# A replicated bias strip written to DRAM in sixteen pieces between the weight chunks, from a work buffer

## The chip, the core and the metric

The kernel runs on one core of a Trainium2 chip. The metric is the device time of one execution in microseconds (us). The kernel before takes 1424.04 us, the median of 3 runs (1423.84 to 1424.34).

## What is computed

The reference is a decoder trunk of two layers on 256 tokens of width 1024, all in float32. A layer has a SwiGLU feed forward, a token mixer and a second feed forward, each followed by a layer norm. The mixer runs sliding-window attention beside a gated delta rule. The change touches one input of the attention: a bias by the distance between query and key, looked up from a table of 32 buckets by 16 heads.

```python
pos_bias = jnp.transpose(rel_bias[t5_bucket(band_rel())], (2, 0, 1)).astype(jnp.float32)
for i in range(DEPTH):
    x = layernorm(DN_ALPHA * x + 0.5 * swiglu(x, ffn_w13[i, 0], ffn_w2[i, 0]), ln_g[i, 0], ln_b[i, 0])
    y = hybrid_mixer(x, w_in[i], ..., pos_bias)
    x = layernorm(DN_ALPHA * x + y, ln_g[i, 1], ln_b[i, 1])
    x = layernorm(DN_ALPHA * x + 0.5 * swiglu(x, ffn_w13[i, 1], ffn_w2[i, 1]), ln_g[i, 2], ln_b[i, 2])
# in the mixer's attention, for a block of 128 queries and 256 keys:
s = jnp.einsum('bqkgd,bskd->bkgqs', qi, ki) + bias
```

## The kernel before

**The weights.** All weights pass through the core once, in 219 chunks of 1 MB (128 partitions by 2048 floats), c0, c1, c2 and so on. c0 to c21 are the first product of layer 0's first feed forward, c22 to c32 its second product, and from c33 on the mixer's. A chunk is loaded by one DMA (L277, in `load_next`; c0 by four), all issued by SP. ACT then rounds it into a high part (CAST, in quarters of 512 columns) and DVE makes the low part, the rest (TENSOR_TENSOR); PE makes each product from three single-pass matmuls of these parts. In the first product a chunk takes 48 matmuls of 256 columns; when they are through, ACT evacuates the bank (ACTIVATE, silu).

**The order of the work.** A Python scheduler writes the instructions of each engine in a fixed order while it keeps its own estimate of each engine's time. Small chains of instructions (generators) are let in between groups of large products. Every engine works through its own list in order, and the waits between engines are semaphores. All DMAs stand in the one list of SP, and so in one hardware queue. `load_next` runs up to three chunks ahead of the conversion and takes its buffer from a pool of 20 slots; another pool, `a`, has 6 work buffers of 1024 columns, which only the mixer uses.

**The strip.** `setup_bias` is such a chain, spawned right after the input has been transposed. It loads the bias table and a one-hot matrix into a buffer `s`, lets PE multiply them, and lets DVE copy the result to a row `r` of 384 columns on 16 partitions, one for each head. Then one DMA (L624) writes `r` 128 times for each head into a DRAM tile `rdram`, at a pitch of 385: 2048 rows of 1536 bytes, 3 MB. Read back at a pitch of 384, each query's row has moved by one. The readers are `att_pair` in the mixer (L1272), two DMAs for each pair of heads, in both layers. In the kernel before `s` is a slot, and the strip is one DMA.

Of the kernel before, what the change touches and what calls it, by code (L numbers as in the profile page):

```python
# [15 lines left out]
P = 128  # L16
# [20 lines left out]
PARTS = 4    # a weight chunk is split in so many steps  # L37
# [4 lines left out]
# column offsets of w_in  # L42
# [3 lines left out]
# head order of the query tiles: a tile holds one head of each partition half  # L46
# [3 lines left out]
def mixer_plan():  # L50
    """Order of the weight chunks of the mixer: (kind, index)."""
    plan = [("z", 0), ("z", 1), ("va", 0)] + [("qa", c) for c in range(5)]
    plan += [(w[:-1], int(w[-1])) for w in ORDER.split()]
    plan += [("wo", c) for c in range(4)]
    return plan
# [18 lines left out]
class Engine:  # L74
    """Issues instructions on one engine and keeps an estimate of when it is through with them.

    Every method takes, first, the estimated time at which its operands are there, and returns the
    estimated time at which its result is. The estimates only settle the order of issue.
    """
# [4 lines left out]
    def __getattr__(self, name):  # L84
        fn, cost = getattr(self.eng, name), self.cost

        def issue(t, *args, **kw):
            fn(*args, **kw)  # L88
            out = kw.get("out", args[0] if args else None)
            self.t = max(self.t, t) + cost(name, out, args, kw)  # L90
            # another function means another table, but for the plain ones
            if name == "activation" and args[2] not in (AF.Copy, AF.Square, self.table):
                self.table = args[2]
                self.t += 1.3
            return self.t + 0.15

        return issue
# [30 lines left out]
class Co:  # L128
    """A chain of small instructions, issued piecemeal between the large products."""
# [5 lines left out]
class Kern:  # L135
    NA = 3      # chunks done one token tile at a time where a phase begins
    LAG = 4     # chunks by which token tile 1 is behind at the end of the second product

    def __init__(self, ctx, tc, a, out):
# [39 lines left out]
        self.lows = deque()  # L179

# [21 lines left out]
    def acq(self, *kinds, dt=F32):  # L202
        """For chains: all of these buffers at once, as soon as they are free."""
        need = {k: kinds.count(k) for k in kinds}
        while any(len(self.pools[k]) < n for k, n in need.items()):
            yield None
        got = [self.new(k, dt) for k in kinds]
        return got[0] if len(got) == 1 else got

    def take(self, kind):  # L210
        """For the main line."""
        self.until(lambda: self.pools[kind])
        return self.new(kind)
# [10 lines left out]
    def tick(self):  # L224
        """Between two groups of large products: whatever small work is ready by now, in turn."""
        ready = [co for co in self.cos if co.wake <= self.T.t]
        n = 0
        while ready:
            again = []
            for co in ready:  # L230
                try:
                    w = next(co.gen)
                except StopIteration as e:
                    co.live, co.end = False, e.value or 0.0
                    self.cos.remove(co)
                    continue
                if w is not None:
                    co.wake = w
                    if w <= self.T.t:
                        again.append(co)  # L240
            ready = again
            n += 1
            assert n < 1000
        self.pump()
# [15 lines left out]
    def after(self, *cos):  # L260
        """For chains: until these others are through."""
        while any(co.live for co in cos):
            yield None
        return max(co.end for co in cos)
# [6 lines left out]
    def load_next(self):  # L271
# [3 lines left out]
        for j in range(n):  # L275
            f = slice(j * SLOT // n, (j + 1) * SLOT // n)
            self.nc.sync.dma_start(out=s[:, f], in_=self.a["wstream"][i, :, f])  # L277
        if self.plan[i][0] == "va":
            self.nc.sync.dma_start(out=self.xps[0], in_=self.a["va7"][self.plan[i][1]])
# [8 lines left out]
    def conv_hi(self):  # L288
        """First operand of the next part of the next chunk."""
# [25 lines left out]
    def pump(self, force=False):  # L315
        i, q = self.ci, self.cp
        n = len(self.plan)
        # two free slots are kept for the split of the next chunk
# [10 lines left out]
    def chunk(self, key):  # L329
        """The two operands of a weight chunk, which is now in use."""  # L330
# [5 lines left out]
    def need(self, key, at):  # L336
        """The chunk is there up to and with this column."""
# [21 lines left out]
    def full_B(self, key, xh, xl):  # L359
        """ps[col, tok] for two column tiles: weights stationary."""  # L360
# [12 lines left out]
    def full_A(self, key, t, n=256):  # L373
        """ps[tok, 0:n]: activations of token tile t stationary, weights moving."""
# [17 lines left out]
    def split(self, t, hi, lo, src):  # L392
        """hi + lo = src, both as single pass operands."""
# [16 lines left out]
    def xT_half(self, tok, q, t):  # L410
        """Transpose and split four column tiles of x."""
# [16 lines left out]
    def ln(self, tok, acc, c, half, last=False):  # L428
        """x[tok] = layernorm(alpha * x[tok] + alpha * c * acc), then its transpose."""
# [48 lines left out]
    def up_A(self, ps, hh, hl):  # L478
        """Evacuates a chunk done for one token tile: silu, gate, transpose."""
# [26 lines left out]
    def ffn(self, l, f, ln_i, first, last):  # L506
# [6 lines left out]
        # the middle group is the short one: it is through before the last chunks of the second product  # L513
# [46 lines left out]
        # token tile 1 is behind in the last chunks, so that the norm of tile 0 is hidden  # L560
# [47 lines left out]
    def setup_bias(self):  # L608
        """Relative bias as a Toeplitz strip in DRAM: R[h, n] = bias at rel = 255 - n."""
        nc = self.nc  # L610
        s = self.alloc()
# [10 lines left out]
        # row q of a head starts 385 * q in: read back at a pitch of 384, it has moved right by q  # L622
        self.rd = self.p_dram.tile([NH_A, P, 385], F32, name="rdram")
        nc.sync.dma_start(out=self.rd[:, :, 0:384], in_=r.unsqueeze(1).broadcast_to([NH_A, P, 384]))  # L624
        self.release(s)


class Mixer:
# [11 lines left out]
    def run(self):  # L640
# [23 lines left out]
        # gates of the norm, and values with the inputs of the decay, one token tile at a time  # L664
# [25 lines left out]
        # the scaled queries take the place of the keys and values of the attention  # L690
# [3 lines left out]
        # sliding window attention  # L694
# [10 lines left out]
        def go(name, *deps):  # L705
            """Spawns a chain as soon as everything that it needs has been issued."""
# [88 lines left out]
    def branch_b(self, c, banks):  # L795
        """Adds the part of four heads to [column, token] of four column tiles.

        Two column tiles share a bank, as one group of accumulation: its start clears the bank, whose
        other columns, marked as not yet written, are overwritten by their first product.
        """  # L800
# [78 lines left out]
    def decay(self):  # L879
# [21 lines left out]
        # log(1 + e) = 2 atanh(y), y = e / (2 + e) <= 1/3  # L901
# [3 lines left out]
        n = 8  # L905
# [11 lines left out]
        # running sums inside each token tile, and the last one of the first  # L917
# [60 lines left out]
    def tok4(self, t, u, tr):  # L978
        """[tok, (t, h), channel] of two heads."""
# [90 lines left out]
    def inverse(self, deps):  # L1070
# [5 lines left out]
        # a partition holds one block: [column half v, row], of the even or the odd columns  # L1076
# [37 lines left out]
        # merge pairs of 32, then the two of 64; U = T^T  # L1114
# [108 lines left out]
    def solved(self, *cos):  # L1223
        """The space of the delta rule goes to the weights."""
# [38 lines left out]
    def att_pair(self, m, *deps):  # L1263
        """Heads 2m and 2m + 1."""
# [4 lines left out]
        # bias: [r, head, own | previous | own]  # L1269
# [24 lines left out]
        # nm = -max(scores, sink), for the two query tiles  # L1294
# [41 lines left out]

def _t5_onehot():
    """[bucket, n]: bucket of the relative distance 127 - n."""
# [11 lines left out]
def _stack_k(w, cols):  # L1350
    """[1024, n] -> [128, 8 * n] with the contraction index on partitions."""
    w = w[:, cols]
    return w.reshape(KD, P, -1).transpose(1, 0, 2).reshape(P, -1)


def _rows(w, c):
    """Two row tiles of a [k, 1024] matrix -> [128, 2048]."""
# [65 lines left out]
```

## Time and profile before

| what | value |
|---|---|
| median of 3 runs | 1424.04 us |
| the profiled execution's span | 1421.5 us |
| PE (matmuls) | 1388.3 us, 98% of the span |
| DVE | 953.7 us, 67% |
| ACT | 754.5 us, 53% |
| DMA queue of the kernel | 245.55 MB, 50.1% of 16 engines |
| the strip, one DMA | 3072.0 KB, 32.8 us from issue to landing |
| granted TensorE clock, mean of the span | 0.99 |

The span is the time from the first to the last instruction of one profiled execution; 2.5 us of the median lie outside it. In the views, PE is the matmul side of TensorE and PEld its weight loads, SPq is SP's own list, and a releaser behind "<-" is what ended an idle time. Nearly all engine instructions carry line L88, since one helper issues them, so they are told apart by operation and tile: `slot<-in_wstream_dram` is a load of weights, `slot<-slot` on ACT the high part, `slot<-slot,slot` on DVE the low part, `bank<-slot,slot` a product, `w<-bank` the evacuation of a chunk of the first product.

### The profile page before, as it was taken

The numbers are of one execution on the slowest core, as the hardware profiler recorded it, in microseconds if no ns is written. First come the engines' busy times: TensorE is split into PE (matmuls) and PEld (weight loads), VectorE is DVE, ScalarE is ACT, GpSimd is POOL, SyncE is SP. The second block draws the span as 40 slices with busy tenths as digits, with TensorE's granted clock in tenths as the row PEclk, the third lists the DMA queues.
The fourth block names the chain that finished last, engine by engine and source line by source line (L and its number), as shares of the span: only waits on it lengthen the run. The fifth ranks groups of instructions, "written<-read, shape, count | busy, mean of one in ns | idle before, by whom it ended". The sixth has DMA issues, their size and how long they took to land.

```text
span 1421.5 us, 26161 instructions
## 1 busy us (share of the span) xinstructions
PE 1388.3 (98%) x10590; PEld 1316.4 (93%) x10590; DVE 953.7 (67%) x2016; ACT 754.5 (53%) x1740; POOL 38.4 (3%) x36
## 2 busy tenths in 40 slices
PE   8599999999999999999999999999999999999997
PEld 7599989889999989999899998898999999899986
DVE  4355567886997696555575555778779778855554
ACT  4344444677566754444444444457774577444441
POOL 0000000000000100000000000000000010000000
PEclk9799999999999999999999999999999999999999
DMA  7964554245533475545654455534444316554560
GB/s 220 255 214 148 207 212 169 98 155 176 186 120 119 144 252 198 179 151 205 237 201 155 151 205 207 194 113 145 170 169 160 135 60 251 204 197 150 183 231 30
DMA packets 46264, 247.21 MB, mean 174 GB/s; under 512 B 5280, under 2 KB 16064, under 8 KB 17856
## 3 DMA queue, kind: packets, MB, share of 16 engines
q1 hardware_dynamic: 46144, 245.55, 50.1%
q8 instruction: 83, 1.36, 0.4%
q14 instruction: 37, 0.30, 0.1%
HBM read 241.34 MB, written 4.19 MB: 173 GB/s over the span
## 4 chain that ended last, share of the span: by engine, by line
PE 95%; DMA 3%; DVE 1%; ACT 0%; SPq 0%; issue 0%; DVEq 0%; ACTq 0%
PE bank L88 95%; DMA slot<-in_wstream_dram 3%; DVE slot L88 1%; ACT slot L88 0%; SPq L591 0%; ACT w L88 0%; DVE bn_st L88 0%; DVEq L1419 0%; DVE w L88 0%; SPq L588 0%; DVE bn_mv L88 0%; DVE bn_rs L88 0%; DVE bd L88 0%; SPq L624 0%; ACTq L88 0%
## 5 line engine op out<-in xcount | busy, mean ns | idle before, releaser
L88 PE MATMUL bank<-slot,slot 128*128 128x256 f32 (+3 forms) x9268 | 1299.1, 300 | 19.9 <-ACT slot L88 18.2
L88 PEld LDWEIGHTS bank<-slot,slot 128*128 128x128 f32 (+1 forms) x9268 | 1212.4, 192 | 82.4 <-ACT slot L88 19.1
L88 DVE TENSOR_TENSOR slot<-slot,slot 128x512 fp32r<-128x512 f32 (+1 forms) x880 | 564.4, 684 | 121.3 <-ACT slot L88 111.1
L88 ACT CAST slot<-slot 128x512 fp32r<-128x512 f32 x872 | 489.1, 619 | 176.5 <-PE bank L88 103.6
L88 ACT ACTIVATE w<-bank 128x256 f32<-128x256 f32 (+1 forms) x97 | 35.4, 365 | 243.8 <-PE bank L88 243.5
L88 DVE TENSOR_TENSOR w<-w,bank 128x256 f32<-128x256 f32 (+1 forms) x97 | 38.4, 396 | 182.1 <-ACT w L88 181.7
L88 ACT CAST slot<-bank 128x512 fp32r<-128x512 f32 (+2 forms) x58 | 24.4, 429 | 51.4 <-PE bank L88 51.3
L88 PE MATMUL bank<-a,slot 128*128 128x128 f32 (+4 forms) x576 | 49.5, 255 | 0.0
L88 PEld LDWEIGHTS bank<-a,slot 128*128 128x128 f32 (+3 forms) x576 | 41.3, 145 | 4.8 <-issue 0.3
L88 DVE TENSOR_TENSOR slot<-bank,slot 128x128 fp32r<-128x128 f32 (+3 forms) x66 | 33.7, 511 | 16.7 <-ACT slot L88 16.5
L88 DVE SCALAR_TENSOR_TENSOR w<-bank,convw,w 128x255 f32<-128x255 f32 (+2 forms) x96 | 41.0, 473 | 2.7 <-ACT w L88 2.4
L88 ACT COPY slot<-bank 128x512 f32<-128x512 f32 (+1 forms) x30 | 16.7, 558 | 47.4 <-PE bank L88 47.4
L88 DVE TENSOR_TENSOR slot<-w,slot 128x256 fp32r<-128x256 f32 x79 | 33.6, 425 | 10.4 <-ACT slot L88 0.7
L88 DVE TENSOR_TENSOR a<-a,a 128x126 f32<-128x126 f32 (+22 forms) x124 | 35.5, 286 | 2.5
L88 DVE SCALAR_TENSOR_TENSOR slot<-bank,slot 128x512 f32<-128x512 f32 x24 | 16.6, 690 | 29.0 <-PE bank L88 28.8
L88 POOL TENSOR_TENSOR bn_rs<-bn_rs,expo 128x1 f32<-128x1 f32 x12 | 11.2, 937 | 869.8 <-DVE bn_rs L88 869.8
L88 ACT ACTIVATE junk<-bank 128x128 f32<-128x128 f32 x96 | 26.6, 277 | 12.4 <-PE bank L88 9.7
L88 ACT CAST slot<-w 128x256 fp32r<-128x256 f32 x79 | 32.0, 405 | 0.6 <-DVE w L88 0.6
L88 ACT COPY a<-bank 128x384 f32<-128x384 f32 (+3 forms) x40 | 20.0, 504 | 20.6 <-PE bank L88 20.5
L88 ACT ACTIVATE a<-a,a_nm 128x128 f32<-128x128 f32 x64 | 28.3, 448 | 4.2 <-DVE a_nm L88 4.2
L88 DVE SCALAR_TENSOR_TENSOR slot<-bank,convw,slot 128x255 f32<-128x255 f32 (+2 forms) x48 | 20.5, 475 | 11.2 <-ACT slot L88 11.2
L88 ACT ACTIVATE slot<-bank 128x256 f32<-128x256 f32 (+2 forms) x22 | 9.7, 440 | 30.5 <-PE bank L88 30.1
(108 smaller groups left out, 564.5 us busy)
## 6 DMA issues: line engine op xcount, KB each, us to landing
slot<-in_wstream_dram SPq DMA_DIRECT2D x215, 1024.0 KB, 4.9
slot<-in_ln_gb_dram SPq DMA_DIRECT2D x6, 1024.0 KB, 6.8
a<-rdram SPq DMA_DIRECT2D x16, 256.0 KB, 4.6
rdram<-slot SPq DMA_DIRECT2D x1, 3072.0 KB, 32.8
a<-rdram SPq DMA_DIRECT2D x16, 128.0 KB, 4.4
slot<-in_x_dram SPq DMA_DIRECT2D x4, 256.0 KB, 3.8
slot<-in_wstream_dram SPq DMA_DIRECT2D x4, 256.0 KB, 6.3
out_dram<-slot SPq DMA_DIRECT2D x4, 256.0 KB, 2.1
```

The costliest lines, as they stand in the source:

```text
L88: fn(*args, **kw)
```

## The change

`setup_bias` takes `s` from the pool of work buffers instead of the slots. It no longer issues the strip: it puts 16 calls into a list, `spread`. Each writes 8 of the 128 rows of every head, 128 rows of 1536 bytes or 192 KB. `load_next` issues one of these calls behind the load of each odd chunk for as long as there are any. The last one gives `s` back. The kernel's other lines in the diff are comments taken out.

```diff
         self.lows = deque()
+        self.spread = deque()
...
             self.nc.sync.dma_start(out=s[:, f], in_=self.a["wstream"][i, :, f])
+        if self.spread and i % 2:
+            self.spread.popleft()()
         if self.plan[i][0] == "va":
...
     def setup_bias(self):
         nc = self.nc
-        s = self.alloc()
+        s = yield from self.acq("a")
         rb, oh, r = s[0:NUM_BUCKETS, 0:NH_A], s[0:NUM_BUCKETS, 128:256], s[0:NH_A, 512:896]
...
         self.rd = self.p_dram.tile([NH_A, P, 385], F32, name="rdram")
-        nc.sync.dma_start(out=self.rd[:, :, 0:384], in_=r.unsqueeze(1).broadcast_to([NH_A, P, 384]))
-        self.release(s)
+
+        n = P // 16
+
+        def piece(q):
+            nc.sync.dma_start(out=self.rd[:, q:q + n, 0:384], in_=r.unsqueeze(1).broadcast_to([NH_A, n, 384]))
+            if q + n == P:
+                self.release(s)
+
+        self.spread += [lambda q=q: piece(q) for q in range(0, P, n)]
```

The lists of PE, DVE, ACT and POOL hold the same instructions in the same order in both kernels; only buffer numbers, and slot against `a` for the strip's operands, differ. SP's list alone changes. Its place at the strip, in the kernel before (slot_211 is c4, slot_261 is c5, and so on up to c11):

```order
L614 DMA slot_139<-in_onehot_dram 32x128
L277 DMA slot_211<-in_wstream_dram 128x2048
L624 DMA rdram<-slot_139 2048x1x384
L277 DMA slot_261<-in_wstream_dram 128x2048
L277 DMA slot_302<-in_wstream_dram 128x2048
L277 DMA slot_356<-in_wstream_dram 128x2048
L277 DMA slot_407<-in_wstream_dram 128x2048
L277 DMA slot_473<-in_wstream_dram 128x2048
```

The same place now (L278 is the load of a chunk, slot_211 is c4, slot_260 is c5; L631 is a piece):

```order
L617 DMA a_139<-in_onehot_dram 32x128
L278 DMA slot_211<-in_wstream_dram 128x2048
L278 DMA slot_260<-in_wstream_dram 128x2048
L631 DMA rdram<-a_139 16x8x384
L278 DMA slot_302<-in_wstream_dram 128x2048
L278 DMA slot_356<-in_wstream_dram 128x2048
L631 DMA rdram<-a_139 16x8x384
L278 DMA slot_408<-in_wstream_dram 128x2048
L278 DMA slot_474<-in_wstream_dram 128x2048
L631 DMA rdram<-a_139 16x8x384
```

c5 has moved ahead of all writing of the strip, and behind it stands a sixteenth of the strip before c6 and c7, and so on by pairs.

Where the pieces end, at the start of the mixer, SP's list before reads as follows (slot_1929 is c35, the values' chunk, with its last columns in spill_w; `a_2467` is the first read of the strip):

```order
L277 DMA slot_1898<-in_wstream_dram 128x2048
L277 DMA slot_1929<-in_wstream_dram 128x2048
L279 DMA spill_w<-in_va_dram 128x272
L277 DMA slot_1984<-in_wstream_dram 128x2048
L277 DMA slot_2026<-in_wstream_dram 128x2048
L645 DMA convw<-in_conv_w_dram 128x96
L647 DMA vec<-in_vec_dram 128x32
L650 DMA dng<-in_vec_dram 128x1
L277 DMA slot_2082<-in_wstream_dram 128x2048
L277 DMA slot_2227<-in_wstream_dram 128x2048
L277 DMA slot_2258<-in_wstream_dram 128x2048
L1272 DMA a_2467<-rdram 128x2x128
```

And now (slot_1943 is c35):

```order
L278 DMA slot_1912<-in_wstream_dram 128x2048
L278 DMA slot_1943<-in_wstream_dram 128x2048
L631 DMA rdram<-a_139 16x8x384
L282 DMA spill_w<-in_va_dram 128x272
L278 DMA slot_1999<-in_wstream_dram 128x2048
L278 DMA slot_2041<-in_wstream_dram 128x2048
L655 DMA convw<-in_conv_w_dram 128x96
L657 DMA vec<-in_vec_dram 128x32
L660 DMA dng<-in_vec_dram 128x1
L278 DMA slot_2097<-in_wstream_dram 128x2048
L278 DMA slot_2242<-in_wstream_dram 128x2048
L278 DMA slot_2273<-in_wstream_dram 128x2048
```

The sixteenth piece stands behind c35 and ahead of its last columns; the first read of the strip follows nine DMAs later, as the next row.

## Rows read from the trace of the kernel before

**Rows 1.** The page: span, PE, granted clock, chain by engine, two DMA issues

```profile
span 1421.5 us, 26161 instructions
PE 1388.3 (98%) x10590; PEld 1316.4 (93%) x10590; DVE 953.7 (67%) x2016; ACT 754.5 (53%) x1740; POOL 38.4 (3%) x36
...
PE 95%; DMA 3%; DVE 1%; ACT 0%; SPq 0%; issue 0%; DVEq 0%; ACTq 0%
...
slot<-in_wstream_dram SPq DMA_DIRECT2D x215, 1024.0 KB, 4.9
...
rdram<-slot SPq DMA_DIRECT2D x1, 3072.0 KB, 32.8
```

**Rows 2.** Chain that ended last, in order: start us, length us, what

```profile
22.84 0.08 SPq L624
22.93 0.04 issue
22.97 35.35 DMA slot<-in_wstream_dram
...
58.39 0.63 ACT slot L88
...
59.06 170.92 PE bank L88 x1168
```

**Rows 3.** Timeline of PE and ACT, 20 to 92: start, us, instruction, [idle before <-releaser]

```profile
21.84 20.42 PE L88 MATMUL bank<-slot,slot 128*128 128x256 f32 x168
59.06 33.12 PE L88 MATMUL bank<-slot,slot 128*128 128x256 f32 x255 [16.80 <-ACT slot L88]
...
30.78 0.38 ACT L88 ACTIVATE w<-bank 128x256 f32<-128x256 f32 x1 [1.96 <-PE bank L88]
58.39 1.14 ACT L88 CAST slot<-slot 128x512 fp32r<-128x512 f32 x2 [27.23 <-DMA slot<-in_wstream_dram]
...
84.65 0.38 ACT L88 ACTIVATE w<-bank 128x256 f32<-128x256 f32 x1 [2.94 <-PE bank L88]
...
90.41 0.38 ACT L88 ACTIVATE w<-bank 128x256 f32<-128x256 f32 x1 [3.00 <-PE bank L88]
```

**Rows 4.** Stretches: length, busy PE PEld DVE ACT POOL, PEclk, DMA share, GB/s

```profile
9.80:18.70 8.90, 8.90 (x50) 8.68 (x51) 4.68 (x8) 4.77 (x7) 0.00 (x0) 1.00 1.02 424
25.00:42.20 17.20, 17.20 (x144) 17.05 (x143) 5.39 (x10) 4.19 (x9) 0.00 (x0) 1.00 0.90 102
42.30:59.00 16.70, 0.00 (x0) 0.00 (x0) 0.00 (x0) 0.61 (x2) 0.00 (x0) 0.63 0.93 194
59.00:62.00 3.00, 2.94 (x12) 2.72 (x13) 2.83 (x5) 3.00 (x8) 0.00 (x0) 0.50 1.02 431
62.00:65.00 3.00, 3.00 (x20) 3.00 (x19) 3.00 (x7) 2.72 (x7) 0.00 (x0) 0.69 1.00 423
65.00:68.00 3.00, 3.00 (x27) 3.00 (x26) 3.00 (x7) 2.23 (x6) 0.00 (x0) 1.00 1.01 426
...
80.00:160.00 80.00, 80.00 (x666) 79.90 (x665) 46.27 (x83) 37.98 (x84) 0.00 (x0) 1.00 0.52 183
160.00:230.00 70.00, 70.00 (x352) 59.60 (x351) 45.62 (x76) 31.64 (x60) 1.98 (x2) 1.00 0.54 188
```

**Rows 5.** SP's own list, 0 to 23; c4's landing us; SP's longest wait

```profile
10.41 0.35 SPq L277 DMA_DIRECT2D slot<-in_wstream_dram  x1
22.26 0.67 SPq L624 DMA_DIRECT2D rdram<-slot  x1
22.97 8.94 SPq L277 DMA_DIRECT2D slot<-in_wstream_dram  x1
...
DMA to landing us min/median/max: 11.2/11.2/11.2
...
SPq L624 <- DVE slot L88: 11.8, 1, 11.8
```

**Rows 6.** Loads of c29, c30, c33 alone: ns, issued at; landing us; ACT's casts

```profile
L277 SPq DMA_DIRECT2D slot<-in_wstream_dram x1: 327/327/327, 173.7 to 173.7; - x1
...
L277 SPq DMA_DIRECT2D slot<-in_wstream_dram x1: 327/327/327, 179.1 to 179.1; - x1
...
DMA to landing us min/median/max: 4.8/4.8/4.8
...
L277 SPq DMA_DIRECT2D slot<-in_wstream_dram x1: 327/327/327, 192.2 to 192.2; - x1
...
DMA to landing us min/median/max: 5.1/5.1/5.1
...
186.53 2.19 ACT L88 CAST slot<-slot 128x512 fp32r<-128x512 f32 x4 [0.94 <-PE bank L88]
...
197.41 4.27 ACT L88 CAST slot<-slot 128x512 fp32r<-128x512 f32 x8 [3.26 <-PE bank L88]
```

**Rows 7.** SP at c35's last columns; reads of the strip: ns, first and last start

```profile
200.96 0.43 SPq L279 DMA_DIRECT2D spill_w<-in_va_dram  x1
...
L1272 SPq DMA_DIRECT2D a<-rdram x32: 359/462/905, 228.7 to 989.5; - x32
```

**Rows 8.** Loads of the input, four of 256 KB: first and last start, landing us

```profile
L591 SPq DMA_DIRECT2D slot<-in_x_dram x4: 420/432/432, 1.2 to 2.6; - x4
...
DMA to landing us min/median/max: 3.2/3.8/4.4
```

## The prediction, on record before the changed kernel ran

> **What bounds the kernel now.** I read the page first. PE is busy for 98% of the span, and 95% of the chain that ended last is PE [rows 1]. So nothing on DVE, ACT or SP is worth anything by itself; only a stretch in which PE stands still can be taken out, and the 3% of DMA in the chain is the one place where another resource holds the end. The strip is the odd row among the DMA issues: 3072 KB in 32.8 us, where a chunk of weights of 1024 KB lands in 4.9 us [rows 1]. The chain in order of time shows where the two meet: SP issues the strip (L624), issues the load of c5 right behind it at 22.97, and that load takes 35.35 us; ACT casts at 58.39 and PE goes on at 59.06 [rows 2]. All DMAs stand in one queue, so c5 waited behind the strip.
>
> PE's timeline shows what that cost: its matmuls of c1 to c4 run to 42.26 (21.84 + 20.42), and then it is idle for 16.80 us until ACT has a quarter of c5 [rows 3]. ACT itself stood for 27.23 us with a cast of c5 at the head of its list [rows 3]. That PE worked on for so long is owed to c1 to c4, which were in SBUF by then.
>
> The stretches add a second loss. While PE stands, the granted clock falls to a mean of 0.63; in the 3 us after it, it is 0.50, which is the lower of the two levels (1.2 against 2.4 GHz), then 0.69, and from 65 on 1.00 [rows 4]. So c5 and a part of the chunks behind it ran at half the speed. After that PE is busy for all of 80 to 230 at 1.00 [rows 4], and the chain has 170.92 us of PE from 59.06 without a break [rows 2]. Whatever time is taken out ahead of 65 should therefore move the whole rest of the program forward.
>
> **What the stall costs in all.** The evacuations are the best clock: ACT's ACTIVATE of a chunk follows the chunk's last matmul. In the undisturbed part they stand 5.76 us apart (90.41 - 84.65) [rows 3]. The one at 30.78 is c2's and the one at 90.41 is c9's, counted in the timeline. Seven chunks at 5.76 are 40.32 us; they took 59.63. The excess is 19.31 us: 16.80 of gap, and 2.51 of low clock. The second part agrees with the stretches: 3 us at 0.50 and 3 us at 0.69 lose 1.5 + 0.9 = 2.4 us.
>
> **The change part by part.**
>
> *c5 goes ahead.* The strip's DMA waited 11.8 us for DVE's copy of `r`, with c5's load behind it [rows 5]. In the new order c5 stands ahead of the first piece. c4 was issued at 10.41 [rows 5]; c5 follows it, and at the 424 GB/s of that stretch [rows 4] its 1.05 MB take 2.5 us of the queue behind c4, which landed at 21.6 (10.4 + 11.2) [rows 5]. It will be there by some 25, and at a pace of 5.76 its cast is due behind c2's evacuation, at about 31. So the gap goes: -16.80. PE then never stands, the clock has no reason to fall: -2.51.
>
> *What is late next.* c6 and c7 stand behind the first piece, which still waits for DVE until 22.26 [rows 5]. A piece is a sixteenth of the strip: 32.8 / 16 = 2.05 us of the queue. c6 lands by about 22.97 + 2.05 + 4.9 = 30 and is cast at about 31 + 5.76 = 36.8, so 7 us to spare; each chunk behind it gains, as the queue moves two chunks and a piece in 2 x 2.47 + 2.05 = 7.0 us (1.05 MB at 424 GB/s is 2.47) while PE needs 11.52 for the two. Neither ends the gap anew.
>
> *Sixteen pieces beside the weights.* They are 15 issues more in SP's list, at 0.67 us as the strip's took [rows 5]; SP has nothing else to do there. Their 32.8 us of queue time do not go away, they are spread to c35, which was issued just ahead of its last columns at 200.96 [rows 7]. The DMA engines are taken 0.52 and 0.54 of that time by now [rows 4]; 32.8 us in some 160 make it 0.73. A piece costs PE something only where a chunk lands less than 2.05 us before its cast. I took issue, landing and cast for each chunk from c9 on; the two tightest are c30 (179.1 + 4.8 = 183.9, cast at 186.53: 2.6 us) and c33 (192.2 + 5.1 = 197.3, its casts being the second half of the row of eight, at about 199.5: 2.2 us) [rows 6]. c33 has c32 between itself and a piece. c30 stands straight behind one in SP's list, but is issued 5.4 us after c29 (173.7) [rows 6], while c29 needs 2.47 of the queue and the piece 2.05. So neither should see even the 2.05. Cost: 0, with the bound taken below.
>
> *The reads of the strip.* The first one is issued at 228.7 [rows 7], some 28 us after c35. The last piece needs 2 us of queue and its landing, so the wait for it is over in time. Cost 0. The same cover holds if all moves forward by 19 us, as both do.
>
> *The work buffer.* `s` in pool `a` is held to c35; the pool's users are in the mixer, and the lists of PE, DVE, ACT and POOL are the same instruction by instruction. The pool of slots has one more free for a while, which moves only the numbers. Cost 0.
>
> **Small transfers.** The four input loads of 256 KB, issued within 1.4 us, land 3.2 to 4.4 us after their issue [rows 8]: the last one 2.6 us behind the first, so 0.87 us apart, although one by itself takes 3.2. Start and end of neighbours overlap. The Trainium skill, DMA: Bandwidth & Descriptors, section Rules for kernel authors, asks for at least 1 MiB in a DMA and speaks against pieces of 192 KB. If that held here as time in the queue, a piece would hold it for 2.05 us and also for the part of an input load's 3.2 us that is no transfer (3.2 less 0.62 at 424 GB/s, 2.6), 4.65 in all. c30 and c33 would then be late by up to 4.65 - 2.6 = 2.05 and 4.65 - 2.2 = 2.45; other chunks have more room. Sum by that: 4.5 us given back. I take 0, by the input loads' spacing, and keep 4.5 for the range.
>
> **The sum.** The profiled span is 1421.5, the median 1424.04; the 2.5 us outside it are not touched. 1421.5 - 19.3 = 1402.2 of span, and 1424.04 - 19.3 = **1404.7 us**.
>
> **The rivals.**
>
> 1. *The gap goes and the clock doesn't come back*, because PE meets a shorter wait at c5 or c6 that lets it fall all the same. Only 16.8 us are gained at the most: 1407.2. Against it stands the 6 to 7 us in which c5 and c6 are early.
>
> 2. *Pieces hold the queue with their ends*, as worked out above: 1404.7 + 4.5 = 1409.2. Against it: the spacing of the input loads.
>
> 3. *The pieces fill the queue: slower.* The strip was one DMA of 2048 rows, a piece is 16 by 8 rows. If a piece is spread over fewer of the 16 DMA engines than the strip was, it takes longer. Two chunks leave 11.52 - 4.95 = 6.57 us of the queue, so a piece up to 6.57 us is hidden. From there each further us costs 16; at 7.8 us the whole gain is gone. On a quarter of the engines a piece would take 8.2 us, and the loss would be 16 x 1.63 = 26.1: 1430.8. Against it: the strip ran at 102 GB/s with a DMA share of 0.90 [rows 4], so all engines took part although its source has 16 partitions, and a piece still has 16 heads outermost.
>
> 4. *No change*: PE would have starved anyhow, for want of weights rather than for the strip. The weights came at 102 GB/s less the strip, that is hardly at all, from 25 to 42, and at 431 as soon as it was through [rows 4]; PE needs 1.05 MB in 5.76 us, 182 GB/s. I see nothing for it.
>
> **How the numbers follow.** Forecast 1404.7: 0.83. Rival 1: 0.06. Rival 2: 0.06. Rival 3: 0.03. Rival 4: 0.02. The upper end of the range takes in rivals 1 and 2: 1409.2. The lower end: the clock's loss is a single observation, and without a profile it may last twice as long; then the gain is 2.5 more: 1402.2. A measurement of this kernel can tell about 0.2%, 2.8 us, from no change. Faster by more than that: 0.83 + 0.06 + 0.06 = 0.95; the same 0.02; slower 0.03.
>
> **What would show it.** In the profile of the changed kernel, PE's matmuls from 21.84 have no idle of more than a us before the mixer, and PEclk is 1.00 from 10 to 230. The evacuations stand 5.76 apart from 25 on, and c9's comes at about 71.1. c5 lands by about 25. Sixteen rows `rdram<-a` of 192 KB stand among the DMA issues, each landing in 3 to 7 us; the DMA share is about 0.7 from 80 to 180. The first read of the strip is issued at about 209, without a wait. The span is about 1402. I am wrong if PE waits for a chunk behind a piece (c6, c30 or c33 first), if a piece takes over 6 us of the queue, or if PE is slower in the same matmuls.

## The result, and the profile after

The changed kernel takes 1403.21 us (median of 4 runs, 1401.87 to 1406.20) where the kernel before takes 1423.94 in the same runs: a ratio of 0.9862, with an interval of 0.9850 to 0.9874 (the two medians alone give 0.9855). The forecast was 1404.7, a ratio of 0.9864. Repeated on another occasion the ratio was 0.9874 (0.9857 to 0.9890).

The page's lines that answer to [rows 1], and the issues of strip and weights:

```profile
span 1400.7 us, 26179 instructions
PE 1383.9 (99%) x10590; PEld 1312.0 (94%) x10590; DVE 954.9 (68%) x2016; ACT 753.8 (54%) x1740; POOL 39.6 (3%) x36
...
PE 98%; DVE 1%; DMA 0%; ACT 0%; issue 0%; SPq 0%; DVEq 0%
...
slot<-in_wstream_dram SPq DMA_DIRECT2D x215, 1024.0 KB, 5.0
...
rdram<-a SPq DMA_DIRECT2D x16, 192.0 KB, 5.5
```

DMA, 3% of the chain before, is at 0%. The sixteen pieces land 5.5 us after their issue in the median, about as long as a chunk five times their size: each stands right behind one, and from c11 on lands 0.5 to 1.0 us after it. The timeline of PE and ACT for the stretch of [rows 3]:

```profile
21.46 172.78 PE L88 MATMUL bank<-slot,slot 128*128 128x256 f32 x1224
...
30.40 0.38 ACT L88 ACTIVATE w<-bank 128x256 f32<-128x256 f32 x1 [1.96 <-PE bank L88]
30.68 1.13 ACT L88 CAST slot<-slot 128x512 fp32r<-128x512 f32 x2
...
64.96 0.38 ACT L88 ACTIVATE w<-bank 128x256 f32<-128x256 f32 x1 [2.94 <-PE bank L88]
...
70.72 0.38 ACT L88 ACTIVATE w<-bank 128x256 f32<-128x256 f32 x1 [3.00 <-PE bank L88]
```

PE runs for 172.78 us from 21.46 on without a break, and ACT's first cast of c5, which had waited to 58.39, starts at 30.68. The evacuations of c2 and c9 are 40.32 us apart, seven times 5.76 exactly, where before they were 59.63 [rows 3]: the 19.31 us are all gone. The stretches of [rows 4] (length, busy PE PEld DVE ACT POOL, PEclk, DMA share, GB/s):

```profile
25.00:42.20 17.20, 17.20 (x146) 17.20 (x144) 11.66 (x21) 9.17 (x21) 0.00 (x0) 1.00 0.90 331
42.30:59.00 16.70, 16.70 (x142) 16.70 (x140) 10.04 (x18) 8.01 (x18) 0.00 (x0) 1.00 0.60 204
59.00:62.00 3.00, 3.00 (x28) 3.00 (x26) 2.10 (x5) 2.74 (x6) 0.00 (x0) 1.00 0.52 164
...
80.00:160.00 80.00, 80.00 (x589) 76.50 (x588) 44.76 (x79) 36.88 (x78) 0.00 (x0) 1.00 0.57 193
160.00:210.00 50.00, 50.00 (x264) 43.02 (x263) 34.80 (x58) 22.60 (x43) 1.98 (x2) 1.00 0.61 208
```

The granted clock is 1.00 in all five. From 25 to 42 the queue moves 331 GB/s, weights and pieces, where it moved the strip alone at 102 [rows 4]. The profiled spans differ by 20.8 us, 1.5 more than the stall. The chains of the two traces say where that comes from. The mixer of layer 1, in the kernel before and in the changed one (start us, length us):

```profile
923.05 306.06 PE bank L88 x2567
```

```profile
903.33 304.52 PE bank L88 x2567
```

The same 2567 matmuls took 1.54 us longer in the one profiled execution of the kernel before; that belongs to the execution and not to the change (the last section). The execution after also starts 0.4 us earlier, and has 0.5 us more behind the last piece of its chain, which cancel. Over the runs the gain is 1.4% and 1.3%, 18 to 21 us.

### The profile page after: what moved, and what is told of

Its sections match the earlier page's. It is cut to its first block, busy times and chain, and to the rows that moved or that the text cites. A ratio compares the mean times of both kernels' runs of the same rounds, so it can differ in the third digit from the quotient of the medians.

```text
span 1400.7 us, 26179 instructions
## 1 busy us (share of the span) xinstructions
PE 1383.9 (99%) x10590; PEld 1312.0 (94%) x10590; DVE 954.9 (68%) x2016; ACT 753.8 (54%) x1740; POOL 39.6 (3%) x36
## 3 DMA queue, kind: packets, MB, share of 16 engines
q1 hardware_dynamic: 46384, 245.55, 49.8%
## 4 chain that ended last, share of the span: by engine, by line
PE 98%; DVE 1%; DMA 0%; ACT 0%; issue 0%; SPq 0%; DVEq 0%
PE bank L88 98%; DVE slot L88 1%; DMA slot<-in_x_dram 0%; ACT slot L88 0%; SPq L594 0%; ACT w L88 0%; DVE bn_st L88 0%; DVEq L1429 0%; DVE w L88 0%; SPq L591 0%; DVE bn_mv L88 0%; DVE bn_rs L88 0%; DVE bd L88 0%
## 5 line engine op out<-in xcount | busy, mean ns | idle before, releaser
L88 ACT CAST slot<-bank 128x512 fp32r<-128x512 f32 (+2 forms) x58 | 24.3, 428 | 51.8 <-PE bank L88 51.7
L88 DVE SCALAR_TENSOR_TENSOR slot<-bank,slot 128x512 f32<-128x512 f32 x24 | 16.6, 690 | 28.9 <-PE bank L88 28.8
L88 DVE SCALAR_TENSOR_TENSOR slot<-bank,convw,slot 128x255 f32<-128x255 f32 (+2 forms) x48 | 20.5, 475 | 11.1 <-ACT slot L88 11.1
```

## The experiments

**The two ties.** In the kernel before, the strip holds c5 twice. c5's load stands behind it in SP's queue. And c5's high part goes into the very slot from which the strip is read, since that slot was given back when the strip had been issued; ACT's list shows a wait for the strip's DMA ahead of that cast. The change cuts both. Three kernels cut one or both, with the strip in a single DMA in each.

*awhole*: the work buffer alone.

```diff
-        s = self.alloc()
+        s = yield from self.acq("a")
```

> One part alone: the kernel before with the strip's operands in a work buffer instead of a slot; the strip is still one DMA of 3 MB ahead of c5 on SP. In the kernel before, ACT's first cast of c5 waits on c5's landing and also on the strip's, since the high part of c5 goes into the slot that the strip is read from. Theory 1 (the queue decides): c5 still lands at about 58, the gap of 16.8 us stays, 1424 us. Theory 2 (the buffer decides): the cast goes on sooner, 1405 us.

Measured: 1424.39 us, ratio 1.0008 (0.9998 to 1.0017). Theory 1. The queue's tie is enough to keep the whole stall. ACT's longest wait up to 80 (us in total, times, longest):

```profile
ACT slot L88 <- DMA slot<-in_wstream_dram: 30.4, 2, 28.0
```

And PE's timeline:

```profile
60.21 20.04 PE L88 MATMUL bank<-slot,slot 128*128 128x256 f32 x149 [17.56 <-ACT slot L88]
```

*actq_slot*: the queue alone. ACT issues the strip on its own DMA queue, still from the slot.

```diff
-        nc.sync.dma_start(out=self.rd[:, :, 0:384], in_=r.unsqueeze(1).broadcast_to([NH_A, P, 384]))
+        nc.scalar.dma_start(out=self.rd[:, :, 0:384], in_=r.unsqueeze(1).broadcast_to([NH_A, P, 384]))
```

> The kernel before with the strip issued by ACT, on its own DMA queue, still as one DMA and still from a slot. The weights are no longer behind it in the queue. Theory 1 (only the queue mattered): c5 lands by about 30, PE never stands, 1404 us. Theory 2 (the slot mattered too): ACT's cast of c5 still waits until the strip has been read from the slot it writes, at 55 or later, as the weights now share the engines with it; the gap of some 13 to 17 us stays, 1418 to 1424 us.

Measured: 1423.78 us, ratio 1.0003 (0.9993 to 1.0012). Theory 2. Its trace, first c5's load alone (ns, issued at; landing us):

```profile
L277 SPq DMA_DIRECT2D slot<-in_wstream_dram x1: 346/346/346, 11.8 to 11.8; - x1
...
DMA to landing us min/median/max: 12.5/12.5/12.5
```

The strip's issue among the DMA issues, then ACT's longest wait, then PE's timeline:

```profile
rdram<-slot ACTq DMA_DIRECT2D x1, 3072.0 KB, 35.8
```

```profile
ACT slot L88 <- DMA rdram<-slot: 26.9, 1, 26.9
```

```profile
59.23 20.94 PE L88 MATMUL bank<-slot,slot 128*128 128x256 f32 x152 [16.51 <-ACT slot L88]
```

c5 is in SBUF at 24.3 (11.8 + 12.5), 34 us earlier than before, and it is of no use: ACT waits 26.9 us for `rdram<-slot`, and PE stands for 16.51 us as ever. Before, the two waits ended within 4 us of each other (the strip landed at 22.26 + 32.8 = 55.1, c5 at 58.3), and a view that names the last releaser showed the second alone.

*actq_a*: both edits together.

> The kernel before with the strip as one DMA, issued by ACT on its own queue, and its operands in a work buffer: neither queue nor slot ties the weights to it, and nothing is cut into pieces. Theory 1 (the stall is the tie of c5 to the strip, not the strip's size): 1403 to 1406 us, as the changed kernel. Theory 2 (a strip in one go starves the weights on the shared DMA engines whichever queue it is in): a chunk of weights needs 10 us or more while it runs, PE waits again, 1412 to 1424 us.

Measured: 1404.21 us, ratio 0.9872 (0.9857 to 0.9887). Theory 1: the changed kernel's time, with nothing cut into pieces. PE's timeline, and the DMA issues from 20 to 70:

```profile
22.42 57.86 PE L88 MATMUL bank<-slot,slot 128*128 128x256 f32 x480
```

```profile
slot<-in_wstream_dram SPq DMA_DIRECT2D x8, 1024.0 KB, 15.1
...
rdram<-a ACTq DMA_DIRECT2D x1, 3072.0 KB, 38.3
```

On PE's row there is no gap from 22.42 to 80, where the view ends. Between 20 and 70 us a chunk needs 15.1 us to land, since it shares the engines with the strip, but it moves, and PE's lead covers it. The Trainium skill says in DMA: Bandwidth & Descriptors, section Issuing engines are not separate DMA queues, that issuing on several engines saves only the time of issue. These runs differ: *awhole* and *actq_a* differ in the issuing engine alone, and take 1424.39 and 1404.21 us. What ACT's queue took away was the order within one queue; from a slot (*actq_slot*) it saved nothing.

**How fine the pieces must be.** The changed kernel with another count (`n = P // 1`, `// 2` and `// 4` for 16), work buffer and place kept.

> The changed kernel with the strip in one piece instead of sixteen, behind c5, operands in the work buffer. Theory (the queue passes nothing until the strip is through): the strip is issued at about 22 and through at about 55, c6 lands at about 58; PE is through with c5 at 47.7, so it stands for 11 us, and the clock falls again for 2.5: 1403 to 1405 and 13.5 is 1417 to 1418.5 us. Rival (c5 ahead of the strip and the work buffer are all that counts, the cutting nothing): 1403 to 1405 us.

Measured: 1419.6 us, ratio 0.9975 (0.9965 to 0.9986).

> The changed kernel with the strip in two pieces of 16.4 us of the queue, behind c5 and c7. By the queue's own times: the first piece runs from about 22 to 38, c6 lands at 42 and c7 at 44, both before PE is through with c5 at 47.7; the second piece holds the queue to 61, c8 lands at about 63.5, and PE needs it at 47.7 + 2 x 5.76 = 59.2. Theory (a piece costs what it exceeds the lead of the load behind it): a gap of some 4 to 5 us at c8 and 1 to 3 us of catching up, 1409 to 1413 us. Rival (the weights queued behind any long DMA are late by all of it): two gaps, over 1415 us. Rival (two pieces are as good as sixteen): 1402 to 1406 us.

Measured: 1410.4 us, ratio 0.9908 (0.9891 to 0.9925).

> The changed kernel with the strip in four pieces of 8.2 us of the queue, behind c5, c7, c9 and c11. By the same times c6 lands at about 33, c8 at 47 and c10 at 60, where PE needs them at 47.7, 59.2 and 70.7. Theory (the lead of the loads decides): no gap, 1402 to 1406 us, as with sixteen. Rival (pieces must be no longer than the 6.6 us that two chunks leave of the queue): late loads at c8 or c10, 1407 us or more.

Measured: 1403.97 us, ratio 0.9864 (0.9850 to 0.9879). PE's rows behind c5 with one piece, with two, and with four:

```profile
58.63 31.57 PE L88 MATMUL bank<-slot,slot 128*128 128x256 f32 x238 [12.04 <-ACT slot L88]
```

```profile
62.95 0.51 PE L88 MATMUL bank<-slot,slot 128*128 128x256 f32 x2 [3.24 <-ACT slot L88]
63.68 36.58 PE L88 MATMUL bank<-slot,slot 128*128 128x256 f32 x290 [0.22 <-DVE slot L88]
```

```profile
21.12 69.14 PE L88 MATMUL bank<-slot,slot 128*128 128x256 f32 x574
```

The gaps are 12.0, 3.2 and 0. The theory holds for the gaps in all three: PE stands when a piece exceeds the lead of the load behind it, and about as long (some 1 us more than worked out with one piece, 1 us less with two). The whole loss is larger, 15.6 and 6.4 us against four pieces, so 3 to 4 us more are lost with each gap. With two pieces the granted clock fell there, as behind the stall of the kernel before:

```profile
62.00:65.00 3.00, 1.83 (x9) 1.62 (x9) 1.93 (x4) 2.72 (x7) 0.00 (x0) 0.82 1.01 426
65.00:68.00 3.00, 3.00 (x18) 3.00 (x18) 3.00 (x7) 2.72 (x8) 0.00 (x0) 0.62 1.02 426
```

How much of this is the clock was not tried here; *warm* below tries it for the kernel before. One piece still gains 0.25% on the kernel before, which is what c5's place ahead of the strip is worth, with the work buffer. By the runs the cutting is worth 14 to 16 us, and four pieces do what sixteen do.

**What a piece costs.** *x4* writes four times as much behind each odd chunk.

```diff
+            m = 3 * n
+            nc.sync.dma_start(out=more[:, 3 * q:3 * q + m, 0:384], in_=r.unsqueeze(1).broadcast_to([NH_A, m, 384]))
```

> The changed kernel with four times the writing: behind each piece a second DMA of 16 by 24 rows from the same operands into a DRAM tile that nobody reads, so that each odd chunk is followed by 768 KB. Theory of the prediction (two chunks leave 6.57 us of the queue, a piece below that is free, beyond that each us costs one per pair): 8.2 us a pair is 1.6 too much, 26 us over the sixteen pairs, less the lead of 12 to 18 us by which loads land before their casts: 1411 to 1420 us. Rival (the queue has more room than that): 1402 to 1406 us. Rival (each piece in the way costs PE its whole time): 98 us more of the queue, over 1480 us.

Measured: 1404.47 us, ratio 0.9872 (0.9859 to 0.9886): the second theory, more room than I gave it. Two stretches (columns as above), ACT's casts of c28 to c34, and the two kinds of piece among the DMA issues:

```profile
80.00:160.00 80.00, 80.00 (x587) 76.39 (x587) 44.30 (x78) 36.90 (x78) 0.00 (x0) 1.00 0.89 244
150.00:190.00 40.00, 40.00 (x178) 33.14 (x177) 22.84 (x38) 17.38 (x32) 0.00 (x0) 1.00 0.96 273
```

```profile
161.08 4.27 ACT L88 CAST slot<-slot 128x512 fp32r<-128x512 f32 x8 [3.26 <-PE bank L88]
169.19 2.19 ACT L88 CAST slot<-slot 128x512 fp32r<-128x512 f32 x4 [3.85 <-DMA slot<-in_wstream_dram]
171.73 2.19 ACT L88 CAST slot<-slot 128x512 fp32r<-128x512 f32 x4 [0.35 <-PE bank L88]
180.20 4.48 ACT L88 CAST slot<-slot 128x512 fp32r<-128x512 f32 x8 [6.28 <-DMA slot<-in_wstream_dram]
191.30 2.18 ACT L88 CAST slot<-slot 128x512 fp32r<-128x512 f32 x4 [6.62 <-DMA slot<-in_wstream_dram]
```

```profile
more<-a SPq DMA_DIRECT2D x16, 576.0 KB, 11.0
rdram<-a SPq DMA_DIRECT2D x16, 192.0 KB, 9.1
```

The queue is full: 0.89 and 0.96 of the engines' time. From c30 on ACT waits for the weights themselves, 3.9 to 6.6 us at a time, so the lead of the loads is used up. c30's cast comes at 169.19 and came at 166.84 in the changed kernel. Yet PE is busy for all of 150 to 190: the casts are made that much ahead of PE's need. The 1411 to 1420 us of the first theory did not come, and the trace shows that the piece was taken too large. ACT waits for c30, c32 and c34 and casts them as they land, at 169.19, 180.20 and 191.30: a pair takes 11.0 to 11.1 us of the full queue, not 13.15 (4.95 + 8.2). Less the two chunks' 4.95, that is 6.1 us for 768 KB, under the 6.57 that the prediction leaves a piece. So its threshold was not passed here; larger pieces and longer strips were not tried.

**The slot and sixteen pieces.** *slot* is the changed kernel with `s = self.alloc()` again.

> The changed kernel with the strip's operands in a slot again, in sixteen pieces as before. No weight's operand is written into that slot while pieces are read from it, since it is given back behind c35 only; instead the weights have one slot less for 180 us, and some loads and casts move a place in their lists. Theory 1 (the work buffer matters for a strip in one go alone): 1402 to 1406 us. Theory 2 (with pieces, the missing slot makes loads late): 1408 us or more.

Measured: 1405.22 us, ratio 0.9876 (0.9863 to 0.9890). Theory 1. With pieces the slot is given back behind c35 only, no weight is written into it while it is read, and one slot less for the weights costs nothing that these runs can tell.

**The clock's share.** *warm* keeps PE busy in the stall of the kernel before.

```diff
         wh, wl = self.chunk(key)
+        if key == ("w13", 0, 0, 5):
+            b = self.take("co")
+            for i in range(136):
+                self.nc.tensor.matmul(b[:, 0:256], lhsT=xh[:, i % KD, 0:P], rhs=xh[:, i % KD, :], start=True, stop=True)
+            self.release(b)
```

> The kernel before, with 136 matmuls of 128x256 more on PE between c4 and c5, on operands that have long been there and into a bank that nobody reads; 136 at 0.12 us fill 16.3 of the 16.8 us in which PE stood. Nothing else changes, c5 still lands at about 58. Theory of the prediction (of the stall's 19.3 us, 16.8 are the gap and 2.5 are the clock, which falls while PE is idle): the clock stays at 1.00 from 42 to 65 and the time is 2.5 us less than that of the kernel before, about 1420.6 to 1421.5 us. Rival (c5 to c8 are slow since ACT and DVE have to catch up, not for the clock): no change, 1423 to 1424 us.

Measured: 1423.22 us, ratio 0.9998 (0.9989 to 1.0007), that is 0.3 us less, between 1.6 less and 1.0 more. Three stretches, PE's timeline, and c9's evacuation on ACT:

```profile
42.30:59.00 16.70, 15.85 (x132) 15.65 (x131) 0.22 (x1) 0.87 (x2) 0.00 (x0) 1.00 0.94 207
59.00:62.00 3.00, 2.59 (x19) 2.18 (x19) 2.87 (x6) 2.92 (x7) 0.00 (x0) 1.00 1.01 426
62.00:65.00 3.00, 3.00 (x28) 3.00 (x27) 3.00 (x7) 2.76 (x6) 0.00 (x0) 1.00 1.00 423
```

```profile
58.80 0.50 PE L88 MATMUL bank<-slot,slot 128*128 128x256 f32 x2 [0.85 <-ACT slot L88]
59.52 0.97 PE L88 MATMUL bank<-slot,slot 128*128 128x256 f32 x6 [0.22 <-DVE slot L88]
60.69 34.58 PE L88 MATMUL bank<-slot,slot 128*128 128x256 f32 x286 [0.19 <-DVE slot L88]
...
88.83 0.38 ACT L88 ACTIVATE w<-bank 128x256 f32<-128x256 f32 x1 [3.00 <-PE bank L88]
```

The clock stays at 1.00, and the kernel hardly gains. PE now waits twice more for DVE's low parts, and the first eight matmuls of c5 take 1.9 us, where the steady pace is 0.12 us each: ACT and DVE have evacuations and casts to catch up on, and a PE at full speed runs into them. In this trace c9 is evacuated 30.0 us after PE's start on c5 (88.83 - 58.80), against 31.35 before (90.41 - 59.06) [rows 3] and 28.8 at the pace of 5.76. So of the 2.5 us behind the gap about half, 1.3, is the clock, and about half the catching up, as far as one trace of each tells; the runs show 0.3 for the clock, and allow up to 1.6.

**The spread of the runs.**

> The changed kernel as it is, again. Both theories: a median of 1402 to 1406 us. The first four runs spread over 4.3 us where those of the kernel before spread over 0.6. Theory A: each execution differs by how often the granted clock falls for some 3.4 us in the mixer's stretches of small matmuls, so that time and mean clock of the runs lie on one line, about 1.7 us for each 0.0012 of the mean clock (half of 3.4 us over 1400). Theory B: they differ by the moments at which pieces and weights meet in the queue; then the clock says nothing about the time.

Measured: 1405.29 us (1402.62 to 1406.88). Neither theory whole. The executions do differ by stretches at half clock, and a single one of them has its price. The chain of this profiled run has the mixer of layer 0, then that of layer 1; below it stands a stretch inside the second:

```profile
212.07 304.52 PE bank L88 x2567
...
903.30 306.12 PE bank L88 x2567
```

```profile
1106.70:1110.10 3.40, 3.40 (x18) 3.40 (x17) 1.91 (x6) 1.98 (x9) 0.00 (x0) 0.50 0.57 239
```

1.60 us for one such stretch. Not every one has a price: the same trace shows 0.50 from 11.0 to 14.4 too, and its mixer of layer 0 starts at 212.07, where that of the other trace of this kernel, without such a stretch, starts at 212.13. And the runs do not lie on one line: 1404.05 and 1406.88 have the same mean clock of 0.996. Over the 20 runs of the changed kernel, x4, slot and four, time and mean clock correlate with -0.62. What makes up the rest of the spread stays open.

## Why the prediction was right, point by point

**The stall's size** was right: 19.31 us from the evacuations, and the evacuations after stand at the undisturbed pace from c2 on. c9 came at 70.72 (forecast 71.1; the whole execution started 0.4 us earlier). The 2.5 us outside the span did not stay untouched: they are 1.8 to 1.9 in all eight runs of the changed kernel, where the runs of the kernel before have 2.3 on average. The forecast has no term for these 0.5 us, and their cause is open.

**c5 ahead of the strip.** c5 was issued at 11.0 and landed 13.1 us later, at 24.1; the forecast was some 25.

```profile
DMA to landing us min/median/max: 13.1/13.1/13.1
```

What I had not seen is that this alone would not have released it. The step on the work buffer, "which moves only the numbers. Cost 0", was wrong as an explanation: with a strip in one go in the slot, c5 can land at 24 and PE still stands (*actq_slot*). The number survived by luck: for no reason that the prediction gave, the change cuts that tie as well, and twice over, by the buffer and by giving it back behind c35 only (*slot*). The profile of before could not show the tie, since the wait for c5 ended later; it stands in the list of waits of the program, which I had read for SP alone and not for ACT's cast.

**The clock's 2.51** was mis-sized as a term: by the traces about 1.3 is the clock and the rest ACT and DVE catching up, by the runs 0.3 and at most 1.6 is the clock (*warm*). The agreement with the stretches (2.4 us at 0.50 and 0.69) was no evidence, because a slow PE hides the waits that a fast one meets. The sum of both goes with the gap, so the forecast did not suffer.

**The pieces cost nothing**: right, and with far more room than the bound of 2.05 us suggested. c30 was issued at 159.4 and landed in 4.7, c33 at 172.5 and in 5.1 (the landings of each alone, then ACT's cast of c30):

```profile
DMA to landing us min/median/max: 4.7/4.7/4.7
...
DMA to landing us min/median/max: 5.1/5.1/5.1
```

```profile
166.84 2.18 ACT L88 CAST slot<-slot 128x512 fp32r<-128x512 f32 x4 [0.94 <-PE bank L88]
```

That is 2.7 us ahead of c30's cast (166.84 - 164.1), as before; the pieces did not touch it.

The term itself, 2.05 us of the queue for a piece, was too large. From c11 on a piece lands 0.5 to 1.0 us behind its chunk. And the strip's 32.8 us did go away in part: the queue's packets took 50.1% of the engines' 1421.5 us before and 49.8% of 1400.7 after, for the same 245.55 MB, 712 and 698 us. Why a piece passes so fast between weights stays open. The deadline was too strict as well: the bound took the cast for the moment at which a chunk is late, and in *x4* casts came later and PE did not stand. One sign was missed: a piece should land in 3 to 7 us, and two of the first three took 9.2 and 7.9.

Rival 2, a price for each piece's start and end, has no support: sixteen pieces (1403.2 and 1405.3), four (1404.0) and one strip on its own queue (1404.2) can't be told apart. Rival 3's first step, a full queue, is seen at four times the piece; its price is not, since 768 KB took 6.1 us of the queue there and not 8.2.

**The DMA share** was forecast at 0.7 from 80 to 180 and was 0.57 to 160, 0.59 to 180. Half of the pieces stand behind c5 to c19 and were through before 100, so only six were issued from 80 to 160; and each took less than 2.05 us. The kernel before at the same place of the program:

```profile
99.40:179.40 80.00, 80.00 (x590) 76.55 (x590) 45.03 (x80) 36.89 (x78) 0.00 (x0) 1.00 0.51 176
```

The six pieces add 0.06 of 80 us, some 0.8 us each.

**The reads of the strip** began at 209.0, as forecast:

```profile
L1282 SPq DMA_DIRECT2D a<-rdram x32: 359/461/1006, 209.0 to 969.8; - x32
L631 SPq DMA_DIRECT2D rdram<-a x16: 345/424/558, 21.9 to 181.3; - x16
```

## What to carry to other kernels

A long transfer that nobody needs soon should not stand in one queue ahead of transfers that PE needs next: cut it so that a piece is shorter than the lead of the load behind it (here four pieces sufficed), or give it a queue of its own. Then look for the second tie: a buffer that the transfer reads from and that is handed out again when the transfer has been issued holds its next writer just as long, and a profile that names the last releaser shows only the later of two waits that end together. A loss behind a stall is not the clock's because the clock is low there; keep the engine busy through the stall and see what comes back.

## What the runs showed of the hardware

A strip of 3 MB read from 16 partitions is hardly faster alone: 32.8 us by itself in SP's queue [rows 1], 38.3 us on ACT's queue with the weight stream beside it. By itself it took 0.90 of the engines' time at 102 GB/s [rows 4]; with weights and pieces in one queue the same share moved 331.

A mixer's 2567 matmuls take 304.5 us or 306.1: in the twelve traces 13 times the one and 11 times the other, and in each of the 11 the granted clock drops to 0.50 once, behind a run of 32x32 matmuls in which PE was busy (to 1106.0, the drop from 1106.7 to 1110.1 above). Whether it drops differs from execution to execution of the same kernel, and it is one part of why runs of the changed kernel spread over 5 us.
